# A hybrid decoder layer on one core: three projection units side by side at the start, and VectorE making one operand sum of the down product

## The chip, the core and the metric

The kernel runs on one core of a Trainium2 chip. Its engines are TensorE (PE in the profile, its weight loads PEld), VectorE (DVE), ScalarE (ACT), GpSimd (POOL) and SyncE (SP); 16 DMA engines move data between the memory of the chip and the core's on-chip buffers. The metric is the time of one execution in microseconds (us), the median of the runs.

## The reference, cut

One layer, batch 1, 512 tokens, width 1024, all in float32:

```python
u = rms_norm(h, ln_mix_pre)
proj = u @ w_in                      # q, k, v of three mixers and the gates
y_swa, y_sb, y_mem = window_attention(...), stick_breaking(...), memory_cross_attention(...)
merged = sum of sigmoid(gate_i) * (y_i @ w_branch_i)
h = h + rms_norm(merged @ w_out, ln_mix_post)
u = rms_norm(h, ln_ffn_pre)
ffn = (silu(u @ w_gate) * (u @ w_up)) @ w_down      # d_ff 2816
out = h + rms_norm(ffn, ln_ffn_post)
```

The change touches the first projections of `u @ w_in`, the order of the gate/up product and the operands of the down product.

## The kernel before

**Products in three passes.** A float32 product is made of three TensorE passes in fp32r. Each operand is split: ScalarE casts it to its high part `hi` (L134), VectorE subtracts that from the operand and has the low part `lo` (L135), and `mm3` (L165 to L168) issues hi by hi, then one high part with the other low part, twice. A weight unit is a column block of 128 outputs over all of K, 128x1024 floats, 512 KB, or eight chunks of K of 128x128.

**Order.** A class `Stream` keeps lists of units and runs their matmuls in order. Ahead of them it issues loads (LOAD_AHEAD, 4 units; 5 in the feed-forward stream) and splits (SPLIT_AHEAD, 3 units), and calls functions hung on a unit's load or split at that point. Each engine runs its instructions in the order in which the program gives them; a tile of a pool is taken again only when its last reader is done. The pool `wp` has three raw buffers of 128x1024 (`raw`) and four each of `hi` and `lo`.

**The beginning** (L481 to L539) is written out by hand under `manual_schedule`. WARM bf16 matmuls on zeros run while the first data come. The input `xT` comes in eight chunks x0 to x7 of 128x512 (`load_x`); `gain_split` (L238, L239) makes of each chunk times the gain `g_pre` its high and low parts `uh` (ScalarE) and `ul` (VectorE). The first two units come in halves of four chunks, the first halves on ScalarE's DMA queue, the others on SP's. Their matmuls go chunk by chunk, unit beside unit. `dn.ahead(3, -1)` loads and `dn.ahead(4, 2)` splits the third unit, which is numbered 2. Then ScalarE squares the eight chunks (L531, L533), GpSimd adds them up in `xacc` (L534, seven additions), and `rstd_of("x")` multiplies `xacc` by ones on TensorE (`ss_x`, `st_x`) for the norm's scale, by which VectorE then scales the units' results (`kb`, four units; `qb` after them).

**Gate and up** are made by Strassen and Winograd's scheme for 2x2 blocks: seven products p1 to p7 instead of eight, each for eleven column groups n, with weight sums `gw` and sums of the activations as factors (B11, B21, T1, N2, N22, T3, T4). The list `seq` (L1216 to L1220) gives the order of the first groups. Banks: p1, p6, p7 and p4 accumulate in gx, p5 and p3 in gy. `g_sum` (L981) makes a weight sum on VectorE when the unit of p6 or p3 (n > 0) is split; `g_end` joins parts `gp` with a bank (L1007) and frees it for the next group.

**The down product** uses the same seven products, each in six units of two tiles of K (the last of one). `dn_issue` (L1091 to L1111) fetches the operands. A buffer `r` of 128x1024 is loaded for p1 (SP, L1101) and then becomes the operand of p5, p6 and p4 in turn, each time by a DMA on GpSimd's queue that adds the next block of `w_down` to it (L1103). The tiles `bp` of 128x512 are loaded for p3 (SP, L1111), become p7's operands by adding DMAs (L1106), and new ones are loaded for p2. The table `early` says how many units ahead of its use each of these is issued. TensorE goes through p1, p5, p6, p3, p7, p2, p4; the results are named x (p1, p6, p7, p4), y (p5, p3) and w (p2) and the left factors `lh`, `ll`.

Of the kernel before, what the change touches and what calls it, by code (L numbers as in the profile page):

```python
# [10 lines left out]
F32 = mybir.dt.float32  # L11
F32R = mybir.dt.float32r
BF16 = mybir.dt.bfloat16
AF = mybir.ActivationFunctionType
ALU = mybir.AluOpType
AX = mybir.AxisListType

P = 128
# [3 lines left out]
KC = D // P  # L22
# [4 lines left out]
SWA, SB, MEM = 0, 1, 2  # L27
LOAD_AHEAD = 4
SPLIT_AHEAD = 3
WARM = 13  # L30


class Stream:
# [12 lines left out]
    def add(self, src, n, mm):  # L46
        self.units.append({"src": src, "n": n, "mm": mm, "load": [], "split": [], "flags": []})
# [56 lines left out]
def tile_kernel(ctx, tc, a):  # L104
    nc = tc.nc
# [9 lines left out]
    wp = first.enter_context(tc.tile_pool(name="wp", bufs=3))  # L115
    cst = first.enter_context(tc.tile_pool(name="cst", bufs=1))

    def ck(name, dt=F32):
        return ckp.tile([P, 512], dt, tag="ck", name=name)
# [4 lines left out]
    def dps(name):  # L124
        return psd.tile([P, 512], F32, tag="d", name=name)
# [6 lines left out]
    def split(raw, hi, lo):  # L132

        ins = nc.scalar.copy(hi, raw)  # L134
        lows = nc.vector.tensor_tensor(lo, raw, hi.bitcast(F32), op=ALU.subtract)  # L135
        if "behind" in st:
            after(ins, st["behind"][0])
            after(lows, st["behind"][1])
        return ins
# [22 lines left out]
    dn = Stream(w_load, w_split)  # L162
# [7 lines left out]
    def mm(out, l, r, start, stop):  # L170
        nc.tensor.matmul(out, l, r, start=start, stop=stop, skip_group_check=True)  # L171
# [27 lines left out]
    def const(name, shape, pool=cst):  # L199
        t = pool.tile(shape, F32, name=f"c_{name}")  # L200
        nc.sync.dma_start(t[:, :], a[name])
        return t
# [33 lines left out]
    def gained(x, g, h, l):  # L236

        nc.scalar.activation(h, x, AF.Identity, scale=g)  # L238
        nc.vector.scalar_tensor_tensor(l, x, g, h.bitcast(F32), op0=ALU.mult, op1=ALU.subtract)  # L239
# [4 lines left out]
    u = [None] * KC  # L244
# [189 lines left out]
    for h in range(2):  # L434
        for q in range(3):
            n = 3 if q < 2 else 2
# [32 lines left out]
    def load_x(k0, k1):  # L469
        for k in range(k0, k1):  # L470
            xk = ck(f"xT{k}")
            nc.sync.dma_start(xk[:, :], a["xT"][:, k, :])
            xraw.append(xk)

    def gain_split(k):
        h, l = ck(f"uh{k}", F32R), ck(f"ul{k}", F32R)
        gained(xraw[k][:, :], g_pre[:, k : k + 1], h[:, :], l[:, :])
        u[k] = (h[:, :], l[:, :])


    raws = [wp.tile([P, 1024], F32, tag="raw", name=f"raw_first{i}") for i in range(2)]  # L481
    his = [wp.tile([P, 1024], F32R, tag="hi", name=f"hi_first{i}", bufs=4) for i in range(2)]
    los = [wp.tile([P, 1024], F32R, tag="lo", name=f"lo_first{i}", bufs=4) for i in range(2)]

    def first_load(i, half):
        kk = slice(half * 4, half * 4 + 4)
        sl = slice(half * 512, half * 512 + 512)
        eng = nc.scalar if half == 0 else nc.sync
        eng.dma_start(raws[i][:, sl], a["w_p"][:, i, kk].rearrange("p k n -> p (k n)"))

    def first_split(i, half):
        sl = slice(half * 512, half * 512 + 512)
        split(raws[i][:, sl], his[i][:, sl], los[i][:, sl])

    with tc.manual_schedule():

        idle = cst.tile([P, 512], BF16, name="idle")
        nc.vector.memset(idle[:, :], 0.0)
        pw = dps("warm")
        for i in range(WARM):  # L500
            mm(pw[:, :], idle[:, :P], idle[:, :], True, True)

        load_x(0, 1)
        first_load(0, 0)
        first_load(1, 0)
        first_table = nc.scalar.preload_act_table_set("natural_log_exp_and_others")
        g_pre = const("g_pre", [P, KC])
        load_x(1, 4)
        first_load(0, 1)
        first_load(1, 1)  # L510
        load_x(4, 8)
        dn.loaded = dn.have = 2
        gain_split(0)
        first_split(0, 0)
        gain_split(1)
        first_split(1, 0)
        gain_split(2)
        gain_split(3)
        first_split(0, 1)
        first_split(1, 1)  # L520
        dn.ahead(3, -1)
        for k in range(4, KC):
            gain_split(k)
        dn.ahead(4, 2)
        gens = [dn.units[i]["mm"](his[i], los[i]) for i in range(2)]
        for k in range(KC + 1):
            for g in gens:
                next(g, None)
        dn.at = 2
        xacc = ck("xacc")  # L530
        nc.scalar.activation(xacc[:, :], xraw[0][:, :], AF.Square)  # L531
        for k in range(1, KC):
            nc.scalar.activation(xraw[k][:, :], xraw[k][:, :], AF.Square)  # L533
            nc.gpsimd.tensor_tensor(xacc[:, :], xacc[:, :], xraw[k][:, :], op=ALU.add)  # L534
        while dn.at < 4:
            dn.piece()
        st["rs"], st["rb"] = rstd_of("x", xacc, S, aps)
        for f in st.pop("waiting"):
            f()  # L539
# [515 lines left out]
    def left_of(g):  # L1055

        if g >= len(units):
            return
        p, c = units[g]
        n = width(c)  # L1060
        if p == "p3":
            sub(sr[c], sr[c], aq[(0, 1)][c], n, ALU.add)
        x = {"p1": aq[(0, 0)], "p5": sq, "p7": aq[(1, 0)], "p2": aq[(0, 1)], "p4": aq[(1, 1)]}.get(p, sr)[c]
        h, l = ck(f"lh{g}", F32R), ck(f"ll{g}", F32R)
        split(x[:, :n], h[:, :n], l[:, :n])
        left[g] = (h, l)
# [10 lines left out]
    rr = {}  # L1077
    rb = {}
# [7 lines left out]
    def wsrc(j, h, k):  # L1086
        return a["w_dn"][:, h, j * HF + k]

    def tiles_of(c):
        return range(2 * c, min(2 * c + 2, HF))  # L1090

    def dn_issue(p, c):

        j, h = {"p1": (0, 0), "p5": (0, 1), "p6": (1, 1), "p3": (1, 1), "p7": (0, 1), "p2": (1, 0), "p4": (1, 0)}[p]
        ks = tiles_of(c)
        if p in ("p1", "p5", "p6", "p4"):
            n = 512 * len(ks)
            src = a["w_dn"][:, h, j * HF + ks[0] : j * HF + ks[-1] + 1].rearrange("p k n -> p (k n)")
            if p == "p1":
                rr[c] = fp.tile([P, 1024], F32, tag="raw", name=f"r{c}")  # L1100
                nc.sync.dma_start(rr[c][:, :n], src)  # L1101
            else:
                nc.gpsimd.dma_start(rr[c][:, :n], src, accum_op=ALU.add)  # L1103
        elif p == "p7":
            for k, t in zip(ks, rb[("p3", c)]):
                nc.gpsimd.dma_start(t[:, :], wsrc(j, h, k), accum_op=ALU.add)  # L1106
            rb[("p7", c)] = rb.pop(("p3", c))
        else:
            rb[(p, c)] = [ck(f"b{p}{k}") for k in ks]
            for k, t in zip(ks, rb[(p, c)]):  # L1110
                nc.sync.dma_start(t[:, :], wsrc(j, h, k))  # L1111

    def dn_got(p, c):
        return lambda: rr[c] if p in ("p1", "p5", "p6", "p4") else rb[(p, c)]
# [46 lines left out]
    def down(g):  # L1161
        p, c = units[g]

        def gen(hi, lo):
            left_of(g + AHEAD_A)
            if (p, c) == ("p1", NCH - 1):
                sub(sr[c], sq[c], aq[(0, 0)][c], width(c))
            if (p, c) == ("p3", 0):
                gain_out.extend(bcast("g_fpost"))
            if c == 0 and p in ("p1", "p5", "p2"):  # L1170
                for i in range(2):
                    bank[(BANK[p], i)] = aps(f"{BANK[p]}{i}")
            if p == "p4" and c >= NCH - LAST:
                held.append((g, (hi, lo)))
                if c < NCH - 1:
                    return
                for i in range(2):
                    for gg, hl in held:
                        dn_mm(gg, i, hl)
                    dn_end(p, i)  # L1180
                return
            for i in range(2):
                dn_mm(g, i, (hi, lo))
                yield 1.36
                if c == NCH - 1:
                    dn_end(p, i)

        return gen
# [26 lines left out]

    fs = Stream(None, f_split, LOAD_AHEAD + 1)  # L1216
    seq = [("p1", 0), ("p2", 0), ("p1", 1), ("p1", 2), ("p2", 1)]
    seq += [("p5", 0), ("p6", 0), ("p3", 0), ("p5", 1), ("p7", 0), ("p6", 1), ("p4", 0)]
    for n in range(1, HF):
        seq += [(p, n) for p in PROD if (p, n) not in seq]  # L1220
    at = {x: i for i, x in enumerate(seq)}
# [22 lines left out]
            load_at(at[(p, n)] - 2, g_plus, n, key, j, j)  # L1244
    for g, (p, c) in enumerate(units):
        fs.add(dn_got(p, c), 512 * len(tiles_of(c)), down(g))

    early = {"p1": 0, "p5": 3, "p6": 3, "p3": 12, "p7": 3, "p2": 4, "p4": 6}
    for p in ("p1", "p3", "p2", "p5", "p6", "p7", "p4"):
        for c in range(NCH):  # L1250
            load_at(len(seq) + units.index((p, c)) - early[p], dn_issue, p, c)

# [133 lines left out]
```

## Time and profile before

| | us |
|---|---|
| median of 3 runs | 821.13 (820.96 to 821.22) |
| the profiled execution, its own time | 820.93 |
| its span in the profile | 819.2 |
| TensorE busy | 806.8 (98%) |
| VectorE busy | 581.2 (71%) |
| ScalarE busy | 440.3 (54%) |
| GpSimd busy | 101.2 (12%) |

The granted clock of TensorE is full in all slices of the page. How to read the rows: the timeline gives start, duration, engine, line and operation, output from inputs, and in brackets the idle time of that engine just before and what released it. A matmul's duration includes its way through the array, so matmuls that follow each other by 0.227 us are shown 0.39 us long. A row of waits gives the total, the count and the longest. "x7" means that rows which follow each other were put together; the time is then that of the whole group. Rows of transfers give the median from issue to landing.

### The profile page before, as it was taken

The numbers are of one execution on the slowest core, as the hardware profiler recorded it, in microseconds if no ns is written. First come the engines' busy times: TensorE is split into PE (matmuls) and PEld (weight loads), VectorE is DVE, ScalarE is ACT, GpSimd is POOL, SyncE is SP. The second block draws the span as 40 slices with busy tenths as digits, with TensorE's granted clock in tenths as the row PEclk, the third lists the DMA queues.
The fourth block names the chain that finished last, engine by engine and source line by source line (L and its number), as shares of the span: only waits on it lengthen the run. The fifth ranks groups of instructions, "written<-read, shape, count | busy, mean of one in ns | idle before, by whom it ended". The sixth has DMA issues, their size and how long they took to land.

```text
span 819.2 us, 12412 instructions
## 1 busy us (share of the span) xinstructions
PE 806.8 (98%) x4755; PEld 706.5 (86%) x4755; DVE 581.2 (71%) x923; ACT 440.3 (54%) x787; POOL 101.2 (12%) x116
## 2 busy tenths in 40 slices
PE   8999999999999999999999999999999999999996
PEld 5889888778788888888888899999999999988785
DVE  5786768556488853774384879877676777778797
ACT  7463757556555542553362567545555544676573
POOL 2603200000000000221003200010000000234200
PEclk9999999999999999999999999999999999999999
DMA  8434524221221223212359946977767662899902
GB/s 266 121 112 147 186 91 128 84 73 52 78 78 53 78 78 102 78 52 79 101 154 368 235 91 161 243 203 195 192 177 194 180 168 79 194 233 241 206 1 102
DMA packets 38027, 115.82 MB, mean 141 GB/s; under 512 B 4656, under 2 KB 5056, under 8 KB 37968
## 3 DMA queue, kind: packets, MB, share of 16 engines
q1 hardware_dynamic: 28800, 85.94, 33.2%
q0 software_dynamic: 8880, 28.56, 18.1%
q8 instruction: 37, 0.61, 0.3%
q10 hardware_dynamic: 288, 0.52, 0.2%
q14 instruction: 22, 0.18, 0.1%
HBM read 111.34 MB, written 3.67 MB: 140 GB/s over the span
## 4 chain that ended last, share of the span: by engine, by line
PE 92%; DMA 3%; DVE 3%; ACT 1%; issue 1%; DVEq 0%; SPq 0%; ACTq 0%
PE g L166 5%; PE g L168 5%; PE g L167 5%; PE gx L166 5%; PE gx L168 5%; PE gx L167 5%; PE z L171 4%; DMA bp<-in_w_dn 3%; PE br L166 3%; PE br L167 3%; PE br L168 3%; PE gy L168 2%; PE gy L166 2%; PE gy L167 2%; PE x L168 2%; PE x L166 2%
## 5 line engine op out<-in xcount | busy, mean ns | idle before, releaser
L134 ACT CAST hi<-raw 128x1024 fp32r<-128x1024 f32 (+2 forms) x65 | 66.9, 1035 | 111.3 <-issue 47.9
L134 ACT CAST hi<-gw 128x1024 fp32r<-128x1024 f32 x77 | 79.9, 1048 | 82.4 <-DVE gw L981 40.7
L135 DVE TENSOR_TENSOR lo<-gw,hi 128x1024 fp32r<-128x1024 f32 x77 | 93.6, 1223 | 33.9 <-ACT hi L134 33.9
L135 DVE TENSOR_TENSOR lo<-raw,hi 128x1024 fp32r<-128x1024 f32 (+2 forms) x65 | 81.5, 1257 | 23.5 <-ACT hi L134 20.6
L166 PE MATMUL g<-uh,hi 128*128 128x512 f32 x192 | 75.6, 394 | 0.0
L168 PE MATMUL g<-uh,lo 128*128 128x512 f32 x192 | 74.8, 390 | 0.0
L167 PE MATMUL g<-ul,hi 128*128 128x512 f32 x192 | 74.7, 389 | 0.0
L288 DVE SCALAR_TENSOR_TENSOR g<-g,rb_x 128x512 f32<-128x512 f32 x24 | 16.4, 689 | 55.4 <-PE g L168 55.3
L963 POOL DMA_DIRECT2D gw<-in_w_gu x27 | 23.4, 905 | 188.0 <-DMA gw<-in_w_gu 77.3
L168 PEld LDWEIGHTS g<-uh,lo 128*128 128x128 f32 x192 | 36.0, 188 | 7.7
L166 PEld LDWEIGHTS g<-uh,hi 128*128 128x128 f32 x192 | 36.1, 188 | 7.4 <-issue 0.3
L167 PEld LDWEIGHTS g<-ul,hi 128*128 128x128 f32 x192 | 36.1, 188 | 7.2
L166 PE MATMUL x<-hi,lh 128*128 128x512 f32 x88 | 34.4, 391 | 1.2 <-ACT lh L134 1.2
L167 PE MATMUL x<-lo,lh 128*128 128x512 f32 x88 | 34.3, 389 | 0.0
L168 PE MATMUL x<-hi,ll 128*128 128x512 f32 x88 | 34.2, 391 | 0.0
L134 ACT CAST hi<-r 128x1024 fp32r<-128x1024 f32 (+1 forms) x24 | 23.5, 981 | 19.8 <-PE y L168 4.7
L135 DVE TENSOR_TENSOR lo<-r,hi 128x1024 fp32r<-128x1024 f32 (+1 forms) x24 | 27.2, 1135 | 8.5 <-ACT hi L134 8.3
L135 DVE TENSOR_TENSOR lo<-bp,hi 128x512 fp32r<-128x512 f32 x33 | 22.9, 723 | 7.6 <-ACT hi L134 7.6
L184 ACT ACTIVATE e<-e 128x384 f32<-128x384 f32 (+1 forms) x48 | 26.9, 561 | 1.5
L134 ACT CAST hi<-bp 128x512 fp32r<-128x512 f32 x33 | 19.5, 620 | 14.9 <-DMA bp<-in_w_dn 8.3
L166 PE MATMUL gx<-T4h,hi 128*128 128x256 f32 x88 | 25.0, 285 | 1.2 <-DVE gp L1007 1.2
L166 PE MATMUL gx<-B11h,hi 128*128 128x256 f32 x88 | 25.1, 285 | 0.2 <-ACT B11h L892 0.2
(546 smaller groups left out, 2619.7 us busy)
## 6 DMA issues: line engine op xcount, KB each, us to landing
gw<-in_w_gu SPq DMA_DIRECT2D x57, 512.0 KB, 5.2
raw<-in_w_p SPq DMA_DIRECT2D x39, 512.0 KB, 3.6
gw<-in_w_gu POOLq DMA_DIRECT2D x27, 512.0 KB, 7.3
r<-in_w_dn POOLq DMA_DIRECT2D x15, 512.0 KB, 9.9
raw<-in_w_br SPq DMA_DIRECT2D x12, 512.0 KB, 3.6
bp<-in_w_dn SPq DMA_DIRECT2D x22, 256.0 KB, 9.0
raw<-in_w_out SPq DMA_DIRECT2D x8, 512.0 KB, 3.7
bp<-in_w_dn POOLq DMA_DIRECT2D x11, 256.0 KB, 14.5
```

The source lines that it names most:

```text
L134: ins = nc.scalar.copy(hi, raw)
L135: lows = nc.vector.tensor_tensor(lo, raw, hi.bitcast(F32), op=ALU.subtract)
L166: nc.tensor.matmul(out, lh, rh, start=start, stop=False, skip_group_check=True)
L167: nc.tensor.matmul(out, lh, rl, start=False, stop=False, skip_group_check=True)
L168: nc.tensor.matmul(out, ll, rh, start=False, stop=stop, skip_group_check=True)
L171: nc.tensor.matmul(out, l, r, start=start, stop=stop, skip_group_check=True)
L184: ins = nc.scalar.activation(*args, **kw)
L288: nc.vector.scalar_tensor_tensor(t[:, :], ps[:, :], s, st["rb"][:, :], op0=ALU.mult, op1=ALU.mult)
L963: nc.gpsimd.dma_start(gw[(n, key)][:, :], g_src(n, i, j), accum_op=ALU.add)
```

## The change

It has three parts.

1. **Beginning.** WARM goes from 13 to 11. Three units instead of two run side by side, their weights in pieces of two, three and three chunks (128x256, 128x384, 128x384). The first pieces go on ScalarE's queue; `g_pre` is first on SP's queue. The first weight piece is split ahead of x0. The stream's first own unit is then number 3; its raw buffer is that of the first unit.
2. **Gate and up.** In `seq`, p3 of group 1 stands ahead of p4 of group 0 instead of behind it.
3. **Down.** The six adding DMAs that made p6's operand are gone. p6's operand is p5's plus the same block of `w_down` that p3 loads into `bp`, so VectorE adds `bp` to `r` (`dn_sum`, eleven additions of 128x512), at the point where p6's unit is split. p3's load is issued 11 units ahead instead of 12.

```diff
--- before.py
+++ after.py
@@ -27,7 +27,7 @@
 SWA, SB, MEM = 0, 1, 2
 LOAD_AHEAD = 4
 SPLIT_AHEAD = 3
-WARM = 13
+WARM = 11
 
 
 class Stream:
@@ -478,18 +478,19 @@
         u[k] = (h[:, :], l[:, :])
 
 
-    raws = [wp.tile([P, 1024], F32, tag="raw", name=f"raw_first{i}") for i in range(2)]
-    his = [wp.tile([P, 1024], F32R, tag="hi", name=f"hi_first{i}", bufs=4) for i in range(2)]
-    los = [wp.tile([P, 1024], F32R, tag="lo", name=f"lo_first{i}", bufs=4) for i in range(2)]
-
-    def first_load(i, half):
-        kk = slice(half * 4, half * 4 + 4)
-        sl = slice(half * 512, half * 512 + 512)
-        eng = nc.scalar if half == 0 else nc.sync
-        eng.dma_start(raws[i][:, sl], a["w_p"][:, i, kk].rearrange("p k n -> p (k n)"))
-
-    def first_split(i, half):
-        sl = slice(half * 512, half * 512 + 512)
+    FIRST = 3
+    PIECE = ((0, 2), (2, 5), (5, 8))
+    raws = [wp.tile([P, 1024], F32, tag="raw", name=f"raw_first{i}") for i in range(FIRST)]
+    his = [wp.tile([P, 1024], F32R, tag="hi", name=f"hi_first{i}", bufs=4) for i in range(FIRST)]
+    los = [wp.tile([P, 1024], F32R, tag="lo", name=f"lo_first{i}", bufs=4) for i in range(FIRST)]
+
+    def first_load(eng, p):
+        k0, k1 = PIECE[p]
+        for i in range(FIRST):
+            eng.dma_start(raws[i][:, k0 * P : k1 * P], a["w_p"][:, i, k0:k1].rearrange("p k n -> p (k n)"))
+
+    def first_split(i, p):
+        sl = slice(PIECE[p][0] * P, PIECE[p][1] * P)
         split(raws[i][:, sl], his[i][:, sl], los[i][:, sl])
 
     with tc.manual_schedule():
@@ -500,33 +501,33 @@
         for i in range(WARM):
             mm(pw[:, :], idle[:, :P], idle[:, :], True, True)
 
-        load_x(0, 1)
-        first_load(0, 0)
-        first_load(1, 0)
+        first_load(nc.scalar, 0)
         first_table = nc.scalar.preload_act_table_set("natural_log_exp_and_others")
         g_pre = const("g_pre", [P, KC])
-        load_x(1, 4)
-        first_load(0, 1)
-        first_load(1, 1)
-        load_x(4, 8)
-        dn.loaded = dn.have = 2
+        load_x(0, 3)
+        first_load(nc.sync, 1)
+        load_x(3, 5)
+        first_load(nc.sync, 2)
+        load_x(5, 8)
+        dn.loaded = dn.have = FIRST
+        first_split(0, 0)
         gain_split(0)
-        first_split(0, 0)
+        for i in range(1, FIRST):
+            first_split(i, 0)
         gain_split(1)
-        first_split(1, 0)
         gain_split(2)
-        gain_split(3)
-        first_split(0, 1)
-        first_split(1, 1)
-        dn.ahead(3, -1)
-        for k in range(4, KC):
-            gain_split(k)
-        dn.ahead(4, 2)
-        gens = [dn.units[i]["mm"](his[i], los[i]) for i in range(2)]
+        for p in (1, 2):
+            for i in range(FIRST):
+                first_split(i, p)
+            for k in range(*PIECE[p]):
+                if u[k] is None:
+                    gain_split(k)
+        dn.ahead(4, 3)
+        gens = [dn.units[i]["mm"](his[i], los[i]) for i in range(FIRST)]
         for k in range(KC + 1):
             for g in gens:
                 next(g, None)
-        dn.at = 2
+        dn.at = FIRST
         xacc = ck("xacc")
         nc.scalar.activation(xacc[:, :], xraw[0][:, :], AF.Square)
         for k in range(1, KC):
@@ -1093,7 +1094,7 @@
 
         j, h = {"p1": (0, 0), "p5": (0, 1), "p6": (1, 1), "p3": (1, 1), "p7": (0, 1), "p2": (1, 0), "p4": (1, 0)}[p]
         ks = tiles_of(c)
-        if p in ("p1", "p5", "p6", "p4"):
+        if p in ("p1", "p5", "p4"):
             n = 512 * len(ks)
             src = a["w_dn"][:, h, j * HF + ks[0] : j * HF + ks[-1] + 1].rearrange("p k n -> p (k n)")
             if p == "p1":
@@ -1109,6 +1110,14 @@
             rb[(p, c)] = [ck(f"b{p}{k}") for k in ks]
             for k, t in zip(ks, rb[(p, c)]):
                 nc.sync.dma_start(t[:, :], wsrc(j, h, k))
+
+    def dn_sum(c):
+        def add():
+            for i, t in enumerate(rb[("p3", c)]):
+                x = rr[c][:, i * 512 : (i + 1) * 512]
+                nc.vector.tensor_tensor(x, x, t[:, :], op=ALU.add)
+
+        return add
 
     def dn_got(p, c):
         return lambda: rr[c] if p in ("p1", "p5", "p6", "p4") else rb[(p, c)]
@@ -1215,7 +1224,7 @@
 
     fs = Stream(None, f_split, LOAD_AHEAD + 1)
     seq = [("p1", 0), ("p2", 0), ("p1", 1), ("p1", 2), ("p2", 1)]
-    seq += [("p5", 0), ("p6", 0), ("p3", 0), ("p5", 1), ("p7", 0), ("p6", 1), ("p4", 0)]
+    seq += [("p5", 0), ("p6", 0), ("p3", 0), ("p5", 1), ("p7", 0), ("p6", 1), ("p3", 1), ("p4", 0)]
     for n in range(1, HF):
         seq += [(p, n) for p in PROD if (p, n) not in seq]
     at = {x: i for i, x in enumerate(seq)}
@@ -1244,9 +1253,11 @@
             load_at(at[(p, n)] - 2, g_plus, n, key, j, j)
     for g, (p, c) in enumerate(units):
         fs.add(dn_got(p, c), 512 * len(tiles_of(c)), down(g))
-
-    early = {"p1": 0, "p5": 3, "p6": 3, "p3": 12, "p7": 3, "p2": 4, "p4": 6}
-    for p in ("p1", "p3", "p2", "p5", "p6", "p7", "p4"):
+        if p == "p6":
+            fs.on_split(dn_sum(c))
+
+    early = {"p1": 0, "p5": 3, "p3": 11, "p7": 3, "p2": 4, "p4": 6}
+    for p in ("p1", "p3", "p2", "p5", "p7", "p4"):
         for c in range(NCH):
             load_at(len(seq) + units.index((p, c)) - early[p], dn_issue, p, c)
```

What it does to the order of instructions, at the three places that count. First SP, which issues the loads at the beginning; a name such as DMAHW7 is a counter of landed transfers, of which there are eight in turn, and DVE in brackets is a wait for VectorE. Before:

```order
L472 DMA xT_122<-in_xT 128x512 [waits DMAHW1_49]
L472 DMA xT_124<-in_xT 128x512 [waits DMAHW2_49]
L472 DMA xT_126<-in_xT 128x512 [waits DMAHW3_49]
L472 DMA xT_128<-in_xT 128x512 [waits DMAHW4_49]
L146 DMA raw_154<-in_w_p 128x1024 [waits DMAHW5_49]
L201 DMA c_g_mem<-in_g_mem 128x8 [waits DMAHW6_49]
L201 DMA c_ident<-in_ident 128x128 [waits DMAHW7_49]
L201 DMA c_ntri<-in_ntri 128x128 [waits DMAHW0_49]
L201 DMA c_negm<-in_negm 128x128 [waits DMAHW1_49]
L547 DMA sinks<-in_sinks 128x8 [waits DMAHW2_49]
L146 DMA raw_156<-in_w_p 128x1024 [waits DMAHW3_49,DVE_49]
```

And after:

```order
L472 DMA xT_130<-in_xT 128x512 [waits DMAHW7_49]
L472 DMA xT_132<-in_xT 128x512 [waits DMAHW0_49]
L472 DMA xT_134<-in_xT 128x512 [waits DMAHW1_49]
L201 DMA c_g_mem<-in_g_mem 128x8 [waits DMAHW2_49]
L201 DMA c_ident<-in_ident 128x128 [waits DMAHW3_49]
L201 DMA c_ntri<-in_ntri 128x128 [waits DMAHW4_49]
L201 DMA c_negm<-in_negm 128x128 [waits DMAHW5_49]
L548 DMA sinks<-in_sinks 128x8 [waits DMAHW6_49]
L146 DMA raw_186<-in_w_p 128x1024 [waits DMAHW7_49,DVE_49]
```

The load of the first whole unit (raw_154, unit 2, before; raw_186, unit 3, after) moved behind the small constants, and now waits for VectorE, that is, for the last `lo` of the first unit. On ScalarE its cast stands ahead of the eight squares in both.

Second ScalarE at the turn from group 0 to group 1 of gate and up; T4h are p4's left factors, gw the weights and their sums, sg a sigmoid. Before, where hi_4858 is p4's weight and hi_4894 the sum for p3:

```order
L134 CAST hi_4858<-gw_4782 128x1024
L892 CAST T4h_3515<-ur_4400 128x2x128
L892 CAST T4h_3515<-ur_4518 128x2x128
L892 CAST T4h_3517<-ur_4400 128x2x128
L892 CAST T4h_3517<-ur_4518 128x2x128
L184 ACTIVATE sg_4854<-gp_4812 128x256
L1001 COPY gp_4887<-gy_4862 128x512
L134 CAST hi_4894<-gw_4297 128x1024
```

And after, where hi_4869 is the sum for p3 and hi_4904 p4's weight:

```order
L893 CAST T4h_3525<-ur_4410 128x2x128
L893 CAST T4h_3527<-ur_4410 128x2x128
L893 CAST T4h_3525<-ur_4528 128x2x128
L893 CAST T4h_3527<-ur_4528 128x2x128
L184 ACTIVATE sg_4864<-gp_4820 128x256
L1002 COPY gp_4898<-gy_4873 128x512
L134 CAST hi_4869<-gw_4307 128x1024
L134 CAST hi_4904<-gw_4832 128x1024
```

The cast of p4's weight moved from ahead of the T4h to behind the cast of p3's sum. On VectorE the sum `gw` moved from behind `lo` and `aq` to right behind the join of gy. TensorE's order there is now two matmuls of p3 (N22 by hi), two of p4 (T4 by hi), the other 22 of p3, the other 22 of p4; before, it was all 24 of p4 and then the 24 of p3.

Third VectorE in the down product, after the change, from p5's first unit on; r_7017 is the operand of the first unit of p1, p5, p6 and p4, ll belongs to a left factor:

```order
L135 TENSOR_TENSOR lo_7279<-r_7017,hi_7278 128x1024 [waits DMASW3_49,Activation_49]
L135 TENSOR_TENSOR ll_7307<-sq_3554,lh_7306 128x512 [waits Activation_49]
L1118 TENSOR_TENSOR r_7017<-r_7017,bp_7248 128x512 [waits DMAHW6_49,DVE_49]
L135 TENSOR_TENSOR lo_7303<-r_7049,hi_7302 128x1024 [waits DMASW4_49,Activation_49]
L135 TENSOR_TENSOR ll_7331<-sq_3555,lh_7330 128x512 [waits Activation_49]
L1054 TENSOR_TENSOR sr_3564<-sq_3558,aq_3534 128x256
L1118 TENSOR_TENSOR r_7017<-r_7017,bp_7249 128x512 [waits DMAHW7_49]
L135 TENSOR_TENSOR lo_7327<-r_7083,hi_7326 128x1024 [waits DMASW5_49,Activation_49]
L1118 TENSOR_TENSOR r_7049<-r_7049,bp_7273 128x512 [waits DMAHW0_49,DVE_49]
L1118 TENSOR_TENSOR r_7049<-r_7049,bp_7274 128x512 [waits DMAHW1_49]
```

The rows of L1118 are new; the others stood there before in the same order, but for the additions sr, which are spread a little differently. On GpSimd the six DMAs into r between p5's six and p4's six are gone.

## Prediction

> **What bounds the kernel now.** I read the page first: busy times, and the line of slices for TensorE.
>
> ```profile
> span 819.2 us, 12412 instructions
> PE 806.8 (98%) x4755; PEld 706.5 (86%) x4755; DVE 581.2 (71%) x923; ACT 440.3 (54%) x787; POOL 101.2 (12%) x116
> PE   8999999999999999999999999999999999999996
> ```
>
> TensorE is busy 806.8 of 819.2 us, and only the first and the last slice are below nine tenths. The change leaves the number of fp32 matmuls as it is, so all that it can win lies in the 12.4 us in which TensorE is idle, and all that it can lose is new idle time. The view of waits, for TensorE alone, names what it waits for.
>
> ```profile
> PE gx L166 <- DVE gp L1007: 1.2, 1, 1.2
> PE x L166 <- ACT lh L134: 1.2, 1, 1.2
> PE kb L166 <- ACT hi_first L134: 0.8, 1, 0.8
> PE kb L168 <- DVE lo_first L135: 0.3, 1, 0.3
> ```
>
> The three edits aim at these rows: the start (hi_first, lo_first), one wait in the gate/up product (gp), one in the down product (lh). Each of the last two is about 0.2% of the span. I take them one by one, in the timeline of the engines concerned.
>
> **The start: the gain.** TensorE's timeline at the beginning, and where it reaches the sum of squares:
>
> ```profile
> 6.45 0.50 PE L166 MATMUL kb<-uh,hi_first 128*128 128x512 f32 x1 [0.78 <-ACT hi_first L134]
> ...
> 8.93 0.40 PE L166 MATMUL kb<-uh,hi_first 128*128 128x512 f32 x1
> 29.35 1.02 PE L171 MATMUL ss_x<-xacc,ones 128*128 128x512 f32 x2
> ```
>
> The matmul at 8.93 is the seventh of the 96 of the four units kb; the 90 from there to 29.35 take 20.42 us, 0.227 each. The first six took 2.48 us instead of 1.36, from 6.45. What sets 6.45 stands in the chain that ended last and in the rows of ScalarE:
>
> ```profile
> 1.17 3.91 DMA c_g_pre<-in_g_pre
> ```
>
> ```profile
> 5.17 0.72 ACT L238 ACTIVATE uh<-xT,c_g_pre 128x512 fp32r<-128x512 f32 x1 [2.24 <-DMA c_g_pre<-in_g_pre]
> 5.79 0.60 ACT L134 CAST hi_first<-raw_first 128x512 fp32r<-128x512 f32 x1
> ...
> 13.69 1.06 ACT L134 CAST hi<-raw 128x1024 fp32r<-128x1024 f32 x1 [0.59 <-DMA raw<-in_w_p]
> 14.64 0.63 ACT L531 ACTIVATE xacc<-xT 128x512 f32<-128x512 f32 x1
> ```
>
> g_pre lands at 5.08, behind x0 in SP's queue, and uh waits for it. After the change g_pre is ahead of x0 and the first weight piece is half as large. I estimate uh at 4.8 (landing of x0, which was ahead of g_pre and so in by 5.08), with the cast of 128x256 (about 0.37 us, on the line through 0.60 for 512 and 1.06 for 1024 columns) already behind it. So the first matmul is ready at 5.5 and ul, which VectorE makes from uh, at 6.2. A chunk then has nine matmuls, 2.04 us, against 0.62 + 3 x 0.3 = 1.5 us of ScalarE and about 1.7 of VectorE: no further gap. The 95 matmuls after the first take 21.6 us, and TensorE reaches ss_x at 27.8 rather than 29.35, give or take 0.5: 1.5 us won. The two fewer warm matmuls end before that and cost nothing.
>
> **The start: what takes its place.** ss_x needs xacc, which GpSimd sums from squares that ScalarE makes after the cast of the next unit (13.69, then 14.64 above). GpSimd's rows and VectorE's beside them:
>
> ```profile
> 15.87 13.09 POOL L534 TENSOR_TENSOR xacc<-xacc,xT 128x512 f32<-128x512 f32 x7 [0.94 <-ACT xT L533]
> ```
>
> ```profile
> L534 POOL TENSOR_TENSOR xacc<-xacc,xT x7: 1295/2150/2259, 15.9 to 26.8; 128x512 f32<-128x512 f32 x7
> ```
>
> ```profile
> 9.78 1.29 DVE L135 TENSOR_TENSOR lo_first<-raw_first,hi_first 128x512 fp32r<-128x512 f32 x2
> 11.05 2.83 DVE L239 SCALAR_TENSOR_TENSOR ul<-xT,c_g_pre,uh 128x512 fp32r<-128x512 f32 x4
> ...
> 19.89 5.69 DVE L135 TENSOR_TENSOR lo<-raw,hi 128x1024 fp32r<-128x1024 f32 x3 [3.88 <-ACT hi L134]
> 26.35 1.46 DVE L135 TENSOR_TENSOR lo<-raw,hi 128x1024 fp32r<-128x1024 f32 x1 [0.78 <-ACT hi L134]
> ```
>
> The seven additions end at 28.96, 0.39 us before TensorE asks: this chain is the next limit, close behind. An addition takes 1.30 us alone and 2.15 beside VectorE's lo<-raw; (13.09 - 7 x 1.295) / 4 makes 1.0 us lost for each of the four lo<-raw that lie beside them. By the Trainium skill, page "SBUF — State Buffer", section "Who interferes with whom", a VectorE instruction with two SBUF inputs and a GpSimd one that reads SBUF exclude each other for a whole instruction; the trace agrees in kind, and full exclusion at 1.23 us each would put the end 0.7 us later than the 1.0 that I use.
>
> Now the chain begins later. The pool of raw weights has three buffers. Before, the first two units left the third free for unit 2, whose load waited for no split. Now the first three take all, and the load of unit 3 waits until VectorE has done the last piece of the first unit. Ahead of that VectorE has five ul (2.83 / 4, 0.70 each), three lo of 256 columns and four of 384, which I estimate from 0.65 for 512 at 0.38 and 0.53: 6.7 us from 4.8 on, so 11.5, where the last lo_first of before ended at 11.07. The load is issued at 11.6. What it then takes lies between the median of these loads on the page and the one load issued at 11.76, when the queue was still full:
>
> ```profile
> raw<-in_w_p SPq DMA_DIRECT2D x39, 512.0 KB, 3.6
> ```
>
> ```profile
> raw<-in_w_p SPq DMA_DIRECT2D x1, 512.0 KB, 4.8
> ```
>
> That is 15.2 to 16.4; I take 15.8 for the queue is half drained. The cast ends 1.0 later, at 16.8, where before the squares began at 14.64; the first addition follows 1.23 after (14.64 to 15.87), at 18.1. Seven additions alone are 9.07 us. Beside them lie the lo of units 4, 5 and 6, whose buffers TensorE frees after the 72 matmuls of the first three units, near 22.3: 3.0 us more, 30.2 in all. A fourth, of unit 7, comes when unit 3 ends at 27.8, and may catch the last addition: 31.2. I take 30.5. **So ss_x stands at 30.5 instead of 29.35, +1.15 us**, with TensorE idle from 27.8 to 30.5. The ends: load quick and three lo, 29.6 (+0.25); load slow and four lo, 31.9 (+2.5). What follows ss_x (rstd, evacuation of kb, qb) moves with it.
>
> **Gate/up: p3 of group 1 ahead of p4 of group 0.** VectorE, ScalarE and TensorE around the wait:
>
> ```profile
> 513.25 1.22 DVE L981 TENSOR_TENSOR gw<-gw,gw 128x1024 f32<-128x1024 f32 x1
> 514.39 0.68 DVE L1007 TENSOR_TENSOR gp<-gp,gx 128x512 f32<-128x512 f32 x1
> ```
>
> ```profile
> 514.56 1.04 ACT L134 CAST hi<-gw 128x1024 fp32r<-128x1024 f32 x1 [1.77 <-DVE gw L981]
> ```
>
> ```profile
> 513.71 0.28 PE L168 MATMUL gx<-N2h,lo 128*128 128x256 f32 x1
> 515.21 0.36 PE L166 MATMUL gx<-T4h,hi 128*128 128x256 f32 x1 [1.22 <-DVE gp L1007]
> ```
>
> Matmuls of 256 columns follow each other by 0.12, so 515.21 is 1.38 us late. p4 writes the bank that p6 just filled and waits for its join gp, which is queued behind the sum gw at 513.25. After the change that sum is made where the lo of p4 stood, 511.78 to 513.0, ScalarE casts it by 514.1, and two matmuls of p3 run at 514.2. The next two in the order are p4's, whose cast now comes behind the other on ScalarE, at 515.1. Then all runs on. By 515.45 four matmuls are done where before there were two: **-0.2 us**. The bounds: the whole 1.38 is won if p4's cast is early, or 0.8 is lost if the lo of the sum (VectorE, 1.22) comes behind p4's.
>
> **Down product.** TensorE's wait in the timeline, and the page's row of the transfers behind it:
>
> ```profile
> 771.66 0.62 ACT L134 CAST hi<-bp 128x512 fp32r<-128x512 f32 x1 [1.24 <-DMA bp<-in_w_dn]
> ...
> 773.22 0.39 PE L168 MATMUL x<-hi,ll 128*128 128x512 f32 x1
> ...
> 774.80 0.50 PE L166 MATMUL x<-hi,lh 128*128 128x512 f32 x1 [1.20 <-ACT lh L134]
> ...
> 775.87 0.40 PE L166 MATMUL x<-hi,lh 128*128 128x512 f32 x1
> ```
>
> ```profile
> bp<-in_w_dn POOLq DMA_DIRECT2D x11, 256.0 KB, 14.5
> ```
>
> ```profile
> DMA packets 7639, 17.91 MB, mean 236 GB/s; under 512 B 848, under 2 KB 848, under 8 KB 7632
> q0 software_dynamic: 4176, 11.54, 78.8%
> ```
>
> The last two rows are of the window 700 to 776 (all queues, then GpSimd's). ScalarE's casts for lh were late because the cast of bp ahead of them in its order had waited for p7's accumulating transfer. From 773.22 to 775.87 stand four matmuls, 0.91 us at their pace, so 1.74 are lost. These transfers take 14.5 us, issue to landing, since the queues are full. Six are removed, 5 x 512 + 256 KB = 2.88 MB, 12 us at 236 GB/s, all ahead of p7's. A wait that needs some 2 us of them is gone. **-1.74 us.**
>
> In their place stand eleven additions on VectorE, 128x512. The nearest row is its own additions sr in 713 to 745, then its busy time by stage, and the wait for the first lo of p6:
>
> ```profile
> L1053 DVE TENSOR_TENSOR sr<-sr,aq 128x512 f32<-128x512 f32 (+1 forms) x6 | 3.8, 640 | 0.0
> ```
>
> ```profile
> 713.00:745.00 32.00, 32.00 (x143) 26.50 (x142) 25.78 (x36) 21.63 (x33) 10.94 (x13) 1.00 1.07 232
> ```
>
> ```profile
> 730.32 1.22 DVE L135 TENSOR_TENSOR lo<-r,hi 128x1024 fp32r<-128x1024 f32 x1
> ```
>
> 11 x 0.64 = 7.0 us stand against 32.0 - 25.8 = 6.2 idle, so VectorE is full here and ends some 1 us late. TensorE wants the lo that ends at 731.54 only in p6's first unit, after 735.37, 3.8 us later, and the later ones have as much. So the cost is nothing while that cover holds; with it gone each microsecond is one on TensorE. The bp that are added land long before, since p3's loads are still issued eleven units ahead.
>
> **Sum.** +1.15 - 0.2 - 1.74 = -0.8 us, on the profiled execution's 820.93: 820.1. That execution is 0.20 below the median of 821.13, so I give **820.3 us**.
>
> **Rivals.** A, slower: unit 3's load takes 4.8 us and a fourth lo falls in; ss_x stands at 31.9, TensorE has been idle for 4.1 us and comes back at a lower clock. The rows of the warm-up tell the price:
>
> ```profile
> 1.35 4.32 PE L171 MATMUL warm<-idle 128*128 128x512 bf16 x13 [1.35 <-DVE idle L498]
> ```
>
> ```profile
> 4.21 1.46 PE L171 MATMUL warm<-idle 128*128 128x512 bf16 x6
> ```
>
> The last six begin at 4.21 (second row, of a narrower window), so the first seven took 2.86, 1.35 more than at the later pace of 0.215. So +2.55 + 1.35 - 0.2 - 1.74 = +2.0: 823.1. No idle time in this trace is long enough to show it; the point from which it decides lies between the 1.22 us of the longest wait above, after which the pace holds, and 4.1. By the Trainium skill, page "TensorE: Matmul & The Clock Gate", section "Why this matters for your kernels", gaps over about 3 us between bursts bring the clock down, and my 2.7 is just under. B: xacc is not late, because the load is issued sooner or the additions lose less; the 1.5 stay won and the sum is -1.55 - 0.2 - 1.74 = -3.5: 817.6, or between this and the forecast when it is a little late, 818.5 in the middle. For it speaks that the wait hangs on a chain of five estimates, against it that the chain had 0.39 us to spare and begins 2 us later. C: the change does not do what it says for p7, because the additions hold VectorE back by what the transfers did before: +1.15 - 0.2 = +0.95, 822.1. Against it speak the 3.8 us. D: p4's wait goes wholly: 819.1.
>
> **Chances.** Forecast 0.5, A 0.12, B 0.2, C 0.1, D 0.08. A measurement of this kernel tells about 0.2%, 1.64 us, from no change. Faster than that (under 819.5) are B, most of D and the forecast's edge: 0.3. Slower is A: 0.12. The rest, 0.58, is within. The range from 818.2 to 822.5 holds the forecast with its bounds, C, D and over half of B; A and the best of B, 0.2, are left out.
>
> **What would show it.** Right: in TensorE's waits ss_x behind GpSimd xacc with 2 to 3 us, hi_first under 0.3, gx at T4 about 1.1, no x behind lh; the cast of the first 128x1024 raw at 15.8; p7's bp in about 8 us. Wrong: no row for ss_x (B), or a granted clock under 1.00 just behind it (A); lo<-r of p6 as a releaser of x (C). What would upset the sum most is the landing of unit 3's weights.

## The result, and the profile after

The changed kernel takes **825.21 us** (median of 6 runs, 824.19 to 825.73) against 821.06 us (6 runs, 820.88 to 821.49): a ratio of 1.0049, 95% interval 1.0036 to 1.0062. It is slower by 4.15 us, where 0.8 less was forecast, and above the range given.

The page of the changed kernel, busy times, then the slices of TensorE and of its granted clock:

```profile
span 823.2 us, 12411 instructions
PE 809.9 (98%) x4753; PEld 709.1 (86%) x4753; DVE 587.6 (71%) x938; ACT 440.9 (54%) x791; POOL 96.5 (12%) x110
...
PE   9899999999999999999999999999999999999996
...
PEclk9899999999999999999999999999999999999999
```

The first slice is fuller than before (9, not 8), the second is not full, and in the second the granted clock is below 9, which no slice of before showed. TensorE's waits in the changed kernel (total, count, longest):

```profile
PE ss_x L171 <- POOL xacc L535: 3.9, 1, 3.9
PE warm L171 <- DVE idle L499: 1.3, 1, 1.3
PE gx L166 <- ACT hi L134: 0.4, 1, 0.4
PE kb L167 <- DVE ul L239: 0.3, 1, 0.3
PE kb L166 <- ACT uh L238: 0.2, 1, 0.2
PE gy L166 <- ACT hi L134: 0.2, 1, 0.2
```

Read it against the same view of before. The waits for hi_first (0.8), gp (1.2) and lh (1.2) are gone, as the change meant; 0.6 us came at the turn of gate/up; and one new wait of 3.9 us, for xacc, is larger than all that went. Its place, in TensorE's timeline:

```profile
28.24 0.39 PE L168 MATMUL kb<-uh,lo 128*128 128x512 f32 x1
32.49 2.04 PE L171 MATMUL ss_x<-xacc,ones 128*128 128x512 f32 x2 [3.87 <-POOL xacc L535]
34.32 1.71 PE L171 MATMUL st_x<-ones,xacc 128*128 128x1 f32 x8
35.89 0.77 PE L166 MATMUL qb<-uh,hi 128*128 128x512 f32 x1
36.46 0.63 PE L167 MATMUL qb<-ul,hi 128*128 128x512 f32 x1
...
39.43 0.39 PE L168 MATMUL qb<-uh,lo 128*128 128x512 f32 x1
39.66 0.39 PE L166 MATMUL qb<-uh,hi 128*128 128x512 f32 x1
```

ss_x took 1.02 us for two before and takes 2.04 now; qb's matmuls follow each other by 0.43 instead of 0.23 until 39.4. The windows of the changed kernel say why (the columns are time, busy time of the five engines, the granted clock, the share of the DMA engines, GB/s):

```profile
28.40:32.40 4.00, 0.23 (x1) 0.00 (x0) 2.52 (x2) 1.04 (x1) 3.92 (x2) 1.00 0.74 226
32.50:39.40 6.90, 6.90 (x18) 5.15 (x19) 3.81 (x9) 1.93 (x5) 4.15 (x8) 0.51 0.15 48
39.40:42.00 2.60, 2.60 (x13) 2.14 (x12) 2.06 (x3) 1.10 (x2) 0.00 (x0) 1.00 0.00 0
```

After the idle time TensorE works for 6.9 us at a granted clock of 0.51. Matching the two traces matmul by matmul gives where the 4 us lie:

| matmul | before, us | after, us | shift |
|---|---|---|---|
| first of kb | 6.45 | 6.00 | -0.45 |
| last of kb | 29.13 | 28.24 | -0.89 |
| first ss_x | 29.35 | 32.49 | +3.14 |
| ninth of qb | 32.95 | 39.43 | +6.48 |
| behind the turn of gate/up | 521.03 | 527.30 | +6.27 |
| behind p7's old wait | 777.51 | 782.00 | +4.49 |
| last | 811.75 | 816.22 | +4.47 |

So the start loses 6.48 (3.14 until xacc is there, 3.34 by the clock), the turn wins 0.21, the down product 1.78. The span grows by 4.0, since it ends 0.5 us sooner behind the last matmul. It does so in all seven traces with part 1 (6.9 to 7.0 us from the last matmul's begin to the end) and in none without (7.2 us or more); why stays open.

### The profile page after: what moved, and what is told of

It is laid out like the page before. It is cut to its first block, busy times and chain, and to the rows that moved or that the text cites. A ratio compares the mean times of both kernels' runs of the same rounds, so it can differ in the third digit from the quotient of the medians.

```text
span 823.2 us, 12411 instructions
## 1 busy us (share of the span) xinstructions
PE 809.9 (98%) x4753; PEld 709.1 (86%) x4753; DVE 587.6 (71%) x938; ACT 440.9 (54%) x791; POOL 96.5 (12%) x110
## 4 chain that ended last, share of the span: by engine, by line
PE 95%; POOL 1%; DMA 1%; ACT 1%; issue 0%; DVE 0%; ACTq 0%; DVEq 0%; POOLq 0%
PE g L166 5%; PE g L167 5%; PE g L168 5%; PE gx L166 5%; PE gx L168 5%; PE gx L167 5%; PE z L171 4%; PE br L167 3%; PE br L166 3%; PE br L168 3%; PE gy L168 3%; PE gy L166 3%; PE gy L167 3%; PE x L167 2%; PE x L166 2%; PE x L168 2%
## 5 line engine op out<-in xcount | busy, mean ns | idle before, releaser
L166 PE MATMUL gy<-N22h,hi 128*128 128x256 f32 x88 | 25.1, 285 | 0.2 <-ACT hi L134 0.2
```

Source lines behind the costliest of these rows:

```text
L166: nc.tensor.matmul(out, lh, rh, start=start, stop=False, skip_group_check=True)
```

## The experiments

All times are medians of runs beside runs of the kernel before, which stood at 821.0 us each time. Theory 1 is: xacc late, then the clock. Each run was to tell it from a rival.

**The three parts apart.** `start_only` takes the edits at the beginning alone:

```diff
-WARM = 13
+WARM = 11
...
+    FIRST = 3
+    PIECE = ((0, 2), (2, 5), (5, 8))
...
-        dn.ahead(4, 2)
+        dn.ahead(4, 3)
```

> Part 1 alone (three units side by side). Theory 1: all of the loss is at the start, xacc late by 3.1 us and the clock lost behind it, about +6.5 us at the tenth qb matmul in the trace of the change, so 827.5 against 821.1. Rival 2: the start costs only the late xacc of +3.1 us, and the rest of the net loss of 4.1 comes from parts 2 and 3: 824.2.

Measured: 827.45 us (5 runs, 826.31 to 828.15), ratio 1.0077 (1.0065 to 1.0090), +6.4. TensorE's row for ss_x in its trace:

```profile
32.27 2.08 PE L171 MATMUL ss_x<-xacc,ones 128*128 128x512 f32 x2 [3.55 <-POOL xacc L535]
```

The same wait and the same slow pair of matmuls: all of the loss is at the start.

`down_only` takes the edits of the down product alone:

```diff
-        if p in ("p1", "p5", "p6", "p4"):
+        if p in ("p1", "p5", "p4"):
...
+        if p == "p6":
+            fs.on_split(dn_sum(c))
```

> Part 3 alone (six adding transfers become eleven VectorE additions). Theory 1: the wait for lh at p7 goes and the additions are hidden, -1.7 us, 819.3, with no wait of x in TensorE's waits. Rival 2: in the changed kernel p7's transfers had more time only because the start was late; alone the wait stays in part, 820 to 821, or VectorE is late with p6's lo and the time is 822.

Measured: 819.18 us (11 runs, 818.93 to 819.78), ratio 0.9979 (0.9970 to 0.9988), -1.8. No wait of x is left in TensorE's waits. Theory 1 holds: the gain does not hang on the late start.

`down_noadd` is `down_only` without the additions on VectorE:

```diff
-        if p == "p6":
-            fs.on_split(dn_sum(c))
```

> Part 3 alone without the eleven additions on VectorE (left out: p6's operand lacks the block of w_down that should be added). Theory 1: the additions are hidden in VectorE's idle time and in the lead of p6's splits, so leaving them out changes nothing: 819.2, as part 3 alone. Rival 2: they hold TensorE's operands or the casts behind them back a little: 818.5 or less.

Measured: 819.00 us (8 runs, 818.70 to 819.08). Eleven additions of 0.69 us in `down_only`, 7.3 us of VectorE's time, cost at most some 0.2 us of the end. That is theory 1 within the spread of the runs.

`seq_only` has the one line of gate/up:

```diff
-    seq += [... ("p6", 1), ("p4", 0)]
+    seq += [... ("p6", 1), ("p3", 1), ("p4", 0)]
```

> Part 2 alone (p3 of group 1 ahead of p4 of group 0). Theory 1: the waits at the turn go from 1.2 us to 0.6 us, so -0.7 us, 820.4. Rival 2: 0.0 or slower, since the sum only changes places with another cast: 821.1 to 822.

Measured: 821.91 us (11 runs, 821.28 to 822.61), ratio 1.0010 (1.0001 to 1.0019), +0.9. Both theories missed: TensorE's last matmul begins at 811.52, 0.23 earlier than before, and yet the end is later. It lies in the last output transfer. The view of transfers over the tail, of before and then of `seq_only`:

```profile
q1 hardware_dynamic: 288, 0.52, 34.4%
issues: line engine op xcount, KB each, median us to landing
out<-fg SPq DMA_DIRECT2D x2, 256.0 KB, 2.0
```

```profile
q1 hardware_dynamic: 288, 0.52, 29.6%
q14 instruction: 1, 0.01, 0.4%
issues: line engine op xcount, KB each, median us to landing
out<-fg SPq DMA_DIRECT2D x2, 256.0 KB, 2.6
```

The median is of two transfers: one took 2.0 us, the last one 3.2. A packet of 8 KB of an instruction queue (q14) stands among its last packets. In the trace of before that packet comes behind the end of the output.

`seq_down` has both parts with the old beginning, and `seq_down_w11` the same with 11 warm matmuls:

```diff
-WARM = 13
+WARM = 11
```

> Parts 2 and 3 with the beginning of before. Theory 1: the sum of what the two did to TensorE alone, -0.2 - 1.8, 819.0. Rival 2: part 2 alone came out 0.9 us slower, though its last matmul was 0.2 us earlier; if that belongs to part 2, 820.1.

> Parts 2 and 3 with the beginning of before, and 11 warm matmuls instead of 13, so that TensorE's program is four instructions shorter. With 13, the last output transfer took 3.1 us instead of 2.0, with one 8 KB packet of an instruction queue among its last packets. Theory 1 (the moment of that packet depends on how far the program is laid out): with it moved, 2.0 us again and 818.9. Rival 2 (it belongs to part 2's order and stays): 819.9.

Measured: 819.88 us (11 runs, 819.61 to 820.33) and 819.73 us (11 runs, 819.64 to 820.95). Rival 2 both times: 0.6 to 0.7 more than part 3 alone, and in both traces the last output transfer takes 3.1 us, with that packet among its last. In the changed kernel, and in all others here without that packet there, it takes 2.0. That the packet is the cause is argued from this coincidence alone; four instructions fewer on TensorE did not move it, and why part 2 brings it there stays open. It is not in the changed kernel's 4.15 us.

**The clock.** `fill18` gives TensorE something to do while it waits:

```diff
+        for i in range(18):
+            mm(pw[:, :], idle[:, :P], idle[:, :], True, True)
         st["rs"], st["rb"] = rstd_of("x", xacc, S, aps)
```

> The changed kernel with 18 bf16 matmuls on zeros, 3.9 us, between the fourth kb unit and ss_x, into a bank that nothing reads. Theory 1: ss_x still waits for xacc until about 32.4 us, but TensorE does not idle, its clock stays full and qb runs at 0.227 us each from the start: 3.3 us less than the change, 821.9. Rival 2: the slow matmuls behind ss_x come from what runs beside them (GpSimd, the loads), not from the idle time: no difference, 825.2.

Measured: 821.63 us (11 runs, 821.14 to 822.73), 3.6 us less than the changed kernel. TensorE's timeline in `fill18`:

```profile
28.18 4.06 PE L171 MATMUL warm<-idle 128*128 128x512 bf16 x18
32.07 1.02 PE L171 MATMUL ss_x<-xacc,ones 128*128 128x512 f32 x2
33.74 0.48 PE L166 MATMUL qb<-uh,hi 128*128 128x512 f32 x1
```

ss_x begins 0.4 us sooner than in the changed kernel (xacc was done at 31.57 in this execution, and the filling matmuls outlast it), takes 1.02 us, and qb follows 1.67 behind it, as before the change. The same instructions of the other engines run beside it. So the 3.3 us behind ss_x come from the idle time, not from the neighbours.

`fill10`, `fill6` and `fill2` are the same with `range(10)`, `range(6)` and `range(2)`, to find how much idle time it takes.

> The changed kernel with 10 bf16 matmuls on zeros, 2.15 us, between the fourth kb unit and ss_x: TensorE idles some 1.8 us. With 6 of them (2.3 us idle in the profiled execution) the runs spread from 819.9 to 826.6. Theory 1 (whether the clock falls depends on where the idle time lies in a window, and an idle time under 2 us is never long enough): all runs within 821 to 823, as with 18. Rival 2 (any idle time at this place can lower the clock): a spread of more than 3 us again.

> The changed kernel with 6 bf16 matmuls on zeros, 1.3 us, between the fourth kb unit and ss_x: TensorE idles some 2.6 us instead of 3.9. Theory 1 (the clock falls only after an idle time between 2.6 and 3.9 us): as with 18 of them, 821.6. Rival 2 (any longer idle time lowers it, in proportion): 823 to 824.

> As fill6 with 2 matmuls, 0.4 us: TensorE idles some 3.4 us. Theory 1 with a limit near 3.4 us that depends on the phase of a window: some runs at 821.6 and some at 825, or all at one of the two. Rival 2 (in proportion): 824.7 with little spread.

| kernel | idle ahead of ss_x, profiled run | median, us | lowest to highest, runs | runs with a mean granted clock of 0.995 or less |
|---|---|---|---|---|
| fill18 | under 0.1 | 821.63 | 821.14 to 822.73, 11 | 0 |
| fill10 | 2.13 | 822.54 | 820.85 to 825.94, 11 | 1 |
| fill6 | 2.27 | 823.54 | 819.92 to 826.59, 12 | 5 |
| fill2 | 3.5 | 825.26 | 819.98 to 826.28, 12 | 9 |
| the change | 3.87 | 825.21 | 824.19 to 825.73, 6 | 6 |

No theory held as written. The idle time is known for the one profiled execution of each kernel; of the others the record has the time and the granted clock, as a mean over the whole execution. Some 7 us at half clock take 0.004 off that mean, and it parts these runs cleanly: those at 0.995 or less took 824.2 us or more, all others 823.7 or less. (Seven of them stand at 0.991, lower than one such stretch makes it; none of these seven was profiled.) So whether the clock falls is a matter of chance, and it fell in more of the runs the less of the gap was filled. The length of the idle time alone does not decide it. In the profiled run of `fill6` 2.27 us passed and the clock stayed full:

```profile
32.02 1.13 PE L171 MATMUL ss_x<-xacc,ones 128*128 128x512 f32 x2 [2.27 <-POOL xacc L535]
```

```profile
30.00:33.00 3.00, 0.98 (x3) 0.50 (x4) 0.85 (x1) 0.00 (x0) 2.90 (x3) 1.00 0.65 216
33.00:36.00 3.00, 3.00 (x19) 2.61 (x18) 2.05 (x3) 1.68 (x4) 2.76 (x7) 1.00 0.11 42
36.00:39.00 3.00, 3.00 (x15) 2.49 (x14) 2.22 (x7) 1.09 (x2) 0.46 (x1) 1.00 0.00 0
```

In that of `fill10`, 2.13 us were enough. Its windows:

```profile
29.00:33.50 4.50, 2.43 (x12) 0.90 (x10) 3.21 (x2) 1.05 (x1) 4.34 (x3) 1.00 0.81 218
33.50:34.50 1.00, 0.93 (x2) 0.49 (x3) 0.00 (x0) 0.00 (x0) 0.90 (x3) 1.00 0.64 184
34.50:41.50 7.00, 7.00 (x22) 5.74 (x21) 5.20 (x12) 2.95 (x6) 3.27 (x7) 0.52 0.06 20
```

The clock is full when TensorE resumes at 33.57, and falls a microsecond later, at 34.81, in the midst of work. Windows laid on its ends give the stretch at 0.50 as 6.82 to 6.83 us in all four traces that have one (the changed kernel, `start_only`, `fill10` and `fill2`), whatever the idle time ahead of it (3.87, 3.55, 2.13 and 3.45 us).

By the Trainium skill, page "TensorE: Matmul & The Clock Gate", section "Part 1: The HAM clock gate", activity is judged over free-running windows of 3413 ns. The late fall and the wide spread fit that; the idle time of a whole window, which the page asks for, was not needed here. By that figure the stretch is two windows long; and the window that ends with the fall at 34.81 began at 31.40, so that it would hold the whole idle time, 31.43 to 33.57. That is an estimate: no trace shows where the windows lie. Not all of this kernel's spread is the clock: in that run xacc was also done 2.0 us later than in `fill18` (33.52 against 31.57).

**The late start of xacc.** `squares_first` moves the squares and additions ahead of unit 3's split:

```diff
+        xacc = ck("xacc")
+        nc.scalar.activation(xacc[:, :], xraw[0][:, :], AF.Square)
+        for k in range(1, KC):
+            nc.scalar.activation(xraw[k][:, :], xraw[k][:, :], AF.Square)
+            nc.gpsimd.tensor_tensor(xacc[:, :], xacc[:, :], xraw[k][:, :], op=ALU.add)
         dn.ahead(4, 3)
...
         dn.at = FIRST
-        xacc = ck("xacc")
-        nc.scalar.activation(xacc[:, :], xraw[0][:, :], AF.Square)
-        for k in range(1, KC):
-            nc.scalar.activation(xraw[k][:, :], xraw[k][:, :], AF.Square)
-            nc.gpsimd.tensor_tensor(xacc[:, :], xacc[:, :], xraw[k][:, :], op=ALU.add)
```

> The changed kernel with the eight squares (ScalarE) and the seven additions (GpSimd) ahead of the split of unit 3 instead of behind it; ScalarE then begins them at about 14.7 us, when x7 is in, rather than at 18.2 behind the cast that waits for unit 3's load. Theory 1 (the late begin of the chain is the cause): xacc is done at about 28, TensorE reaches ss_x at 28.5 without a wait, no loss of clock, the gain at the start of 0.9 us stays: 821.0 - 0.9 - 0.2 - 1.8 = 818.1. Rival 2 (the contention of the additions with VectorE's lo is the cause, wherever they begin): xacc still ends after 31, and the time is 821 or more.

Measured: **817.61 us** (5 runs, 817.46 to 817.66), ratio 0.9955 (0.9943 to 0.9967). It beats both kernels, by 7.6 and 3.4 us. GpSimd's and TensorE's rows:

```profile
16.01 12.12 POOL L529 TENSOR_TENSOR xacc<-xacc,xT 128x512 f32<-128x512 f32 x7
```

```profile
28.34 1.02 PE L171 MATMUL ss_x<-xacc,ones 128*128 128x512 f32 x2
```

The additions end at 28.13, 0.2 us ahead of TensorE. They are still slowed beside VectorE (12.12 us, not 9.1). Of the 4.3 us by which xacc is done sooner than in the changed kernel, 3.4 are their earlier begin, and 0.9 that they take less. Theory 1 holds to 0.5 us.

## Why the prediction was wrong, point by point

**What bounds the kernel, and the two later parts: right.** TensorE is the bound, the start, the turn and p7's wait were the places. The turn was put at -0.2 and gave -0.21, with both casts in ScalarE's order as described. Only the sign named for it was out: the wait of gx at T4 is 0.4 us, not 1.1. The row of p3, which now begins the turn:

```profile
520.68 0.39 PE L166 MATMUL gy<-N22h,hi 128*128 128x256 f32 x1 [0.19 <-ACT hi L134]
```

The down product was put at -1.74 and gave -1.78 (-1.84 alone). VectorE was nearly as full as worked out, 30.57 us of 32.0:

```profile
717.00:749.00 32.00, 32.00 (x143) 26.50 (x142) 30.57 (x44) 21.37 (x33) 6.01 (x7) 1.00 0.73 162
```

One sentence there was wrong in size: p7's transfers did not fall from 14.5 us to about 8.

```profile
bp<-in_w_dn POOLq DMA_DIRECT2D x11, 256.0 KB, 12.6
```

```profile
GB/s 0 37 238 249 275 243 254 245 249 244 246 244 329 191 2 0 0 0 47 155 164 209 205 201 179 248 235 250 264 264 262 265 260 225 261 259 265 263 266 114
```

The second row has 40 slices of the window 704 to 780: for four of them, from 731 to 738, next to nothing moves. The freed time became a hole, because p4's adding transfers wait for p6's split of r, and behind them the queue is full again. The transfer that had held the wait landed at 771.63 before and at 775.12 now, with TensorE 6.27 us later: it is 2.8 us earlier against TensorE, where 1.74 were needed.

**The start: the step that failed is "ss_x stands at 30.5 instead of 29.35, +1.15 us".** It stands at 32.49, +3.14. And "What follows ss_x (rstd, evacuation of kb, qb) moves with it" failed too: what follows lost another 3.34 us at the lower clock, so that the price is 6.48 us. Term by term:

- TensorE ready for ss_x: put at 27.8, measured 28.47. uh began at 5.23, not 4.8. x0 takes 4.0 us from issue to landing in both kernels, but is issued at 1.17 instead of 0.72, since g_pre now stands ahead of it on SP's queue; the forecast took its landing from before.
- Unit 3's load: put at 11.6, issued at 12.70. VectorE made the last piece of the first unit from 11.86 to 12.41 (put: by 11.5). SP's load waits for x5 as well (its counter, DMAHW7): x5 was issued at 8.04 and took 4.6 us, and its uh began at 12.64. The forecast had not counted x5; which of the two came last, the trace does not tell for certain. The load took 4.5 us instead of 4.2.
- So the squares began at 18.18, not 16.8, and the first addition at 19.41, not 18.1 (1.23 behind the squares, as put).
- The additions took 13.03 us, not 12.4: the fourth lo, of unit 7, did fall in (29.51 below).

```profile
11.86 1.49 DVE L135 TENSOR_TENSOR lo_first<-raw_first,hi_first 128x384 fp32r<-128x384 f32 x3
...
23.42 5.70 DVE L135 TENSOR_TENSOR lo<-raw,hi 128x1024 fp32r<-128x1024 f32 x3 [3.89 <-ACT hi L134]
29.51 1.80 DVE L135 TENSOR_TENSOR lo<-raw,hi 128x1024 fp32r<-128x1024 f32 x1 [0.40 <-ACT hi L134]
```

```profile
17.22 1.05 ACT L134 CAST hi<-raw 128x1024 fp32r<-128x1024 f32 x1 [2.48 <-DMA raw<-in_w_p]
18.18 0.63 ACT L532 ACTIVATE xacc<-xT 128x512 f32<-128x512 f32 x1
```

```profile
19.41 13.03 POOL L535 TENSOR_TENSOR xacc<-xacc,xT 128x512 f32<-128x512 f32 x7 [3.50 <-ACT xT L534]
```

The additions began 1.3 us later than put and took 0.6 longer, so ss_x came 1.99 us later than put. That alone would have made 820.3 into 822.3, inside the range. The rest is the clock, +3.34, which the forecast had at nothing, less the 0.5 us by which the span ends sooner.

**Rival A is what happened**, at a chance of 0.12: load late, a fourth lo, TensorE idle for 3.87 us (4.1 was said) and back at a lower clock. Its price for the clock, 1.35 us from the warm-up, was too small: the slow stretch here is 6.8 us, of which half is lost. The warm-up was no measure of it. Eleven warm matmuls took 4.46 us in the changed kernel, thirteen 4.32 before, and the granted clock reads 1.00 over both:

```profile
1.35 4.46 PE L171 MATMUL warm<-idle 128*128 128x512 bf16 x11 [1.35 <-DVE idle L499]
```

At the full 3.34 A would have stood at 825.1, 0.1 from the median. That nearness is partly luck, for its wait was 0.6 us short and the 0.5 us at the end were in nobody's sum. Its deciding point was badly set too. The forecast's own 2.7 us of idle time was treated as safe; in the profiled run of `fill10` 2.13 us were enough, so even with every term right the forecast would have stood at about 820 or 824 by chance. As an estimate, 2.7 us lies between the profiled idle times of `fill6` and `fill2`, where 5 and 9 of 12 runs lost the clock, so the fall deserved a chance near one half.

**Rival B** (xacc not late) is what `squares_first` makes true; put at 817.6, measured 817.61, though the head start is 1.0 rather than 1.5 us. TensorE's last matmul is 3.0 us earlier than before, and the other 0.5 us come from the end of the span. That they fill the gap of the head start is luck. **C and D** did not happen: `down_only` gave 1.8 us, and the turn 0.21.

What to see in the profile of before: GpSimd's additions ended 0.39 us ahead of TensorE. The forecast saw this and still took the middle of every term, where the price of being late is not linear.

## What to carry to other kernels

When a head start on the bounding engine is won by taking a buffer, look for the chain that used this buffer and how long ahead of its reader it ends; here it was 0.39 us, and the change delayed it by 3.5. On an engine that runs in order, put the work whose data are there ahead of the instruction that waits for a load: moving eight squares past one cast was worth 7.6 us. Price an idle time of TensorE of 2 us or more with the clock behind it: here 3.4 us, times a chance that went from 1 run of 11 to 6 of 6.

## What the runs showed of the hardware

The granted clock of TensorE fell to 0.50 for 6.83 us after 3.87 us of idle time, and for as long in a run with 2.13 us, where it fell a microsecond after work had resumed; in another run 2.27 us of idle time left it at 1.00. Filling 3.9 us with 18 matmuls on zeros kept it at 1.00, and the time was 3.6 us lower. GpSimd's addition of 128x512 took 1.3 us alone and 2.1 to 2.3 beside VectorE's lo. One packet of 8 KB of an instruction queue stood beside a last output transfer of 3.1 to 3.2 us instead of 2.0, in three kernels of three where it came at that moment.
